# Projections of q, k, gate and v as 2x2x2 block products with seven products in place of eight

## The chip, the cores and the metric

One core of a Trainium2 chip runs the program. The metric is the device time of one execution in microseconds (us). TensorE (PE) multiplies, VectorE (DVE), ScalarE (ACT) and GpSimd (POOL) do the rest, SyncE (SP) starts most transfers. Each engine works off its own list of instructions in a fixed order.

## The reference

One layer of a hybrid trunk over 2048 rows of width 1024, all in float32. Cut to what matters:

```
hn   = rmsnorm(x, mix_norm_g)                    # 2048 x 1024
proj = hn @ w_in                                 # 1024 x 3072
u, g_ssm, q, k, v, g_attn = split(proj, 6 x 512)
y_ssm = s5_branch(u) * silu(g_ssm)               # diagonal complex SSM, scan, GELU, GLU
qh, kh = rmsnorm per head of 64                  # 8 heads
z = qh kh^T / 8, strictly causal, blocks of 128 queries
weights = exp(log_sigmoid(z) + sum of log_sigmoid(-z) over later keys)
y_att = (weights @ v) * silu(g_attn)
h = x + concat(y_ssm, y_att) @ w_out
out = h + sigmoid(rmsnorm(h, ple_norm_g) @ w_ple_gate) * (p @ w_ple_proj)
```

The change concerns `proj` without u: 2048 rows by 1024 times 1024 by 2560.

## The kernel before

A float32 product is made of three matmuls: each operand is split into a high part `hi` (a cast on ACT) and the remainder `lo` (a subtraction on DVE), and `mm3` or `mm3x` adds hi·hi, hi·lo and lo·hi in PSUM. 

The program has four stages:

- **u** (`phase_u`): RMSNorm of 16 row blocks of 128, the projection u, and the normalised rows, transposed and split, to DRAM as `hn_d` (1 MB a row block, hi and lo).
- **SSM**: eight batches (`ssm_pack`, `ssm_batch`). Beside each batch stands a `gate_unit`, which makes silu(g_ssm) for 256 rows with 96 matmuls of 256 columns. The last ones are followed by the first four row blocks of the attention projections. Six of the eight batches make their table `stC` (L332 to L334) on POOL, two on DVE.
- **Attention**: 40 steps `t`. The eight heads are four pairs `hp`, and pair `hp` starts at step 8·hp, so two pairs are under way at most times. `attn_block` (scores `ps_z`, DVE scan `px`, transposes `ps_wt`, ACT copy `ws`, output `ps_o`) does block t - 8·hp, and `attn_proj` makes the row block two steps ahead. At t = 30 to 39 the 16 GLU units (`ps_g`, `ps_v`) and, from t = 32, eight `cross_sums` are added: these make sums of blocks of `w_out` and `w_ple_gate` on POOL in tiles `old`, for the last stage.
- **out** (`phase_out`): both products with 1024x1024 weights, each already as 2x2x2 block products with seven products (`cross_products`).

`attn_proj` for one pair and one row block: one transfer of 1 MB from `hn_d` (`xt`, L717), 24 products of 128x128 by 512 columns, and `qn`, a 128x512 tile with q, k, gate and v of two heads. In 60 of the 64 row blocks each product is cut into two matmuls of 64 rows of the array, which run side by side into two PSUM tiles `ps_q` (L745); ACT copies the first (`part`, L751), DVE adds the second (`qn`, L65). In the first four blocks the whole array is used (`ps_qk`). v is shifted down by one row with two transfers (L753, L755) and subtracted on POOL.

The shape of a TensorE matmul is called its use of the array below: `ps_z`, `ps_wt`, `ps_tq` and `ps_q` take row halves (64*128 in the profile), `ps_o` takes column halves (128*64), and projections with the whole array are 128*128.

The order on each engine is not the order of the code. `arrange` passes all instructions with a cost for each through `best_order` and `list_schedule`, which build a list schedule, improve it in some turns and write the instructions in that order; a list cannot be changed at run time. Pools of SBUF are placed by `plan`.

Of the kernel before, what the change touches and what calls it, by code (L numbers as in the profile page):

```python
# [18 lines left out]
P = 128  # L19
# [21 lines left out]
XB, XTB, GTB, QSB, PXB, WSB, SWB, ROTB, STA, STB, STC, ALT, ALT0, ALT1, SSM_STEPS, SSM_DEPTH, PREP0, PXX, WSX, XTX, XT0 = 4, 2, 5, 5, 8, 5, 2, 2, 3, 2, 3, "o", 0, 30, 10, 2, 0, 0, 0, 0, 13  # L41
WE = 6
AHEAD = 4
BANKS = (("z0", "z1", "tr"), ("acc", "ssm"), ("o",)), (("z0", "z1"), ("acc", "tr"), ("o",)), (("z0", "z1"), ("acc", "ssm", "tr"), ("o",))
# [262 lines left out]
def ssm_pack(e, sm, R, b):  # L307
# [23 lines left out]
    gp = (nc.vector if b < 2 else nc.gpsimd).tensor_tensor  # L331
# [16 lines left out]
    lt = e.spare.tile([P, 512], F32, tag="part", name="lt", bufs=1)[:, :HS * P]  # L348
# [124 lines left out]
def load_w(e, blocks, width, scale, tag="w", pool=None, bufs=None, at=0, act=True, spare=None):  # L473
# [3 lines left out]
    for c, src in enumerate(blocks, at):  # L477
        t = (pool or e.wpool).tile([P, 2, width], F32R, tag=tag, name=f"w_{tag}", **({"bufs": bufs} if bufs else {}))
# [67 lines left out]
def phase_u(e, pool, xp, chain):  # L546
# [5 lines left out]
    def load_plain(T):  # L552
        xt = xp.tile([P, 2, 2, NC8, P], F32R, tag="xg", name="xt", bufs=2)
        w = []
        for hf in range(2):
            plain.append(pool.tile([P, NC8, P], F32, tag="x", name="x", bufs=XB))
        for c in range(0, NC8, 2):
            cs = slice(c, c + 2)
            for hf in range(2):
                x = plain[2 * T + hf]  # L560
                nc.sync.dma_start(x[:, cs], e.xt[2 * T + hf, :, cs])
                split(e, xt[:, hf, 0, cs], xt[:, hf, 1, cs], x[:, cs])
            if T == 0:
                w += load_w(e, row_blocks(e.w_in[0], NC8, 0)[cs], 512, e.gmix, act=ACT0, spare=pool, at=c)
        for hf in range(2):
            with e.later(1):
                nc.sync.dma_start(e.hn_d[2 * T + hf], xt[:, hf].rearrange("p s c t -> p (s c t)").bitcast(F32))
        return xt, w
# [19 lines left out]
    def load_x(T):  # L588
        xt = xp.tile([P, 2, 2, NC8, P], F32R, tag="xg", name="xt", bufs=2)
        for hf in range(2):  # L590
# [7 lines left out]
            nc.scalar.activation(x, x, AF.Copy, scale=rs)  # L598
            for h, ps in enumerate(turned(e, "ps_x", ("z0", "z1"), [x[:, c * P:(c + 1) * P] for c in range(NC8)])):
                d = slice(64 * h, 64 * h + 64)  # L600
                split(e, xt[:, hf, 0, :, d], xt[:, hf, 1, :, d], ps)
            nc.sync.dma_start(e.hn_d[2 * T + hf], xt[:, hf].rearrange("p s c t -> p (s c t)").bitcast(F32))
# [10 lines left out]
    for T in range(NT // 2):  # L613
        if 2 <= T + 1 < NT // 2:
            xts[T + 1] = load_x(T + 1)
        xt = xts.pop(T - 2, None)
# [25 lines left out]
def gate_unit(e, pool, w, T, xt):  # L642

    nc = e.nc
    if xt is None:
        xt = pool.tile([P, 2, 2, NC8, P], F32R, tag="xg", name="xg", bufs=2)
        for hf in range(2):
            nc.sync.dma_start(xt[:, hf].rearrange("p s c t -> p (s c t)").bitcast(F32), e.hn_d[2 * T + hf])
    for ct in range(4):
        o = e.bank("ps_sg", "o", "z0", "z1")[:, :256]  # L650
        for c in range(NC8):
            cs = slice(ct * P, (ct + 1) * P)
            mm3(e, o, (w[c][:, 0, cs], w[c][:, 1, cs]), (xt[:, :, 0, c], xt[:, :, 1, c]), c == 0, c == NC8 - 1)
        if T < 1:
            og = pool.tile([P, 256], F32, tag="sg", name="og", bufs=2)
            vt(nc, og, o, e.row[T], ALU.mult)
            o = og
        sg = pool.tile([P, 256], F32, tag="sg", name="sg", bufs=2)
        nc.scalar.activation(sg, o, AF.Sigmoid)
        vt(nc, sg, o, sg, ALU.mult)  # L660
        c0 = (T % 2) * 256
        nc.sync.dma_start(e.gs_d[T // 2][ct * P:(ct + 1) * P, c0:c0 + 256], sg)
    return xt


def glu_load(e, k):
    rows = e.w_glu[0].rearrange("(g h) n -> h g n", h=GH)
    return load_w(e, [rows[4 * c:4 * c + 4, :, 512 * k:512 * k + 512] for c in range(4)], 512, None)


def glu_z(e, pool, tb):

    zf = e.z_d.rearrange("j (k p) c -> p k j c", p=P)
    zr = pool.tile([P, 2, 4, 512], F32R, tag="zr", name="zr", bufs=1)
    for k in range(4):
        n = NCH // 4
        zt = pool.tile([P, L, n], F32, tag="zt", name="zt", bufs=3)
        e.nc.sync.dma_start(zt, zf[:, k, :, tb * n:(tb + 1) * n])
        hi, lo = (zr[:, s, k].rearrange("p (c j) -> p c j", j=L) for s in range(2))
        split(e, hi, lo, zt.rearrange("p j c -> p c j"))  # L680
    return zr


def glu_unit(e, old, slots, w, zr, tb, m):
    nc = e.nc
    both = old(slots[m % len(slots)])
    gt, sg = both[:, 0], both[:, 1]
# [4 lines left out]
    for half, ps in ((1, pg), (0, pv)):  # L692
        for c in range(4):
            wt = w[half][c]
            mm3(e, ps, (wt[:, 0, cs], wt[:, 1, cs]), (zr[:, 0, c], zr[:, 1, c]), c == 0, c == 3)
# [16 lines left out]
def attn_proj(e, pool, A, i, xt=None):  # L712

    nc = e.nc
    if xt is None:
        xt = e.xp.tile([P, 2, NC8, P], F32R, tag="xt", name="xt", bufs=XTB)
        e.xdma(xt.rearrange("p s c t -> p (s c t)").bitcast(F32), e.hn_d[i])  # L717
    both = pool.tile([P, 4 * HPP, HD], F32, tag="qn", name="qn", bufs=2)
    if i == 0:
        A.v[i] = e.kv_tile(A.hp, i, "v", [P, HPP, HD])  # L720
        nc.gpsimd.memset(A.v[i][:1], 0.0)
    if i + 1 < NT and i + 1 not in A.v:
        A.v[i + 1] = e.kv_tile(A.hp, i + 1, "v", [P, HPP, HD]) if i + 1 != AHEAD else pool.tile([P, HPP, HD], F32, tag="vl", name="vl", bufs=1)
    if A.v[i].tensor.name.startswith("vl"):
        row = A.v[i]
        A.v[i] = e.kv_tile(A.hp, i, "v", [P, HPP, HD])
        nc.sync.dma_start(A.v[i][:1], row[:1])
    flat, vb = both.rearrange("p h d -> p (h d)"), A.v[i].rearrange("p h d -> p (h d)")
    vr = flat[:, 384:]
    if len(e.q_banks) == 1:  # L730
        pq = e.bank("ps_qk", *e.q_banks)
        for c in range(NC8):
            mm3x(e, pq, (xt[:, 0, c], xt[:, 1, c]), (A.w[c][:, 0], A.w[c][:, 1]), c == 0, c == NC8 - 1)
        if i < 2:
            nc.scalar.activation(flat, pq, AF.Copy, scale=e.rs[i])
        else:
            nc.scalar.activation(flat, pq, AF.Copy)
    else:
        pq = [e.bank("ps_q", *e.q_banks) for h in range(2)]
        for c in range(NC8):  # L740
            with e.abreast():
                for s, (a, b) in enumerate(((0, 0), (0, 1), (1, 0))):
                    for h, o in enumerate(pq):
                        r = slice(64 * h, 64 * h + 64)
                        nc.tensor.matmul(o, xt[r, a, c], A.w[c][r, b], start=c + s == 0, stop=c == NC8 - 1 and s == 2)  # L745
        part = pool.tile([P, 512], F32, tag="part", name="part", bufs=1)
        if i < 2:
            nc.scalar.activation(part, pq[0], AF.Copy, scale=e.rs[i])
            stt(nc, flat, pq[1], e.rs[i], part, ALU.mult, ALU.add)
        else:  # L750
            nc.scalar.activation(part, pq[0], AF.Copy)  # L751
            vt(nc, flat, pq[1], part, ALU.add)
    nc.sync.dma_start(vb[1:], vr[:P - 1])  # L753
    if i + 1 < NT:
        nc.sync.dma_start(A.v[i + 1][:1].rearrange("p h d -> p (h d)"), vr[P - 1:])  # L755
    nc.gpsimd.tensor_tensor(vb, vr, vb, op=ALU.subtract)  # L756
# [19 lines left out]
    if len(e.q_banks) == 1:  # L776
# [73 lines left out]
def attn_pass(e, hp):  # L850
    A = Env()
    A.hp, A.k, A.v, A.q, A.w = hp, [], {}, {}, []
    return A


def attn_w(e, A, lo, hi, **kw):
    cols = e.w_in[0][:, 1024:].rearrange("(n p) (k c) -> n p k c", p=P, k=4)
    A.w += load_w(e, [cols[c, :, :, P * A.hp:P * (A.hp + 1)] for c in range(lo, hi)], 512, e.gmix, at=lo, **kw)
# [23 lines left out]
class Halves:  # L882
    def __init__(self, e):
        self.e, self.open = e, []

    def tile(self, shape, dt, **kw):
        if not self.open:
            t = self.e.xp.tile([P, 2, NC8, P], dt, tag="xt", name="wx", bufs=XTB)
            self.open = [t[:, k].rearrange("p c t -> p (c t)").rearrange("p (s n) -> p s n", s=2) for k in (1, 0)]
        return self.open.pop()  # L890
# [147 lines left out]
def phase_out(e, pool, far, wpool2, wo4):  # L1038
# [6 lines left out]
    e.wg = [cross_weights(e, e.w_pg[0], e.sg_d, e.gple, p, **(dict(pool=Halves(e)) if p == 4 else dict(tag="wc", pool=wpool2, bufs=8) if p > 4 else {})) for p in range(7)]  # L1045
# [5 lines left out]
def hybrid_block_kernel(ctx: ExitStack, tc: tile.TileContext, x, xt, small, p, w_in, ssm_w_glu, w_out, w_ple_gate,  # L1051
# [15 lines left out]
    e.hn_d = [scratch(f"hn{i}", [P, 2 * DM]) for i in range(NT)]  # L1067
# [96 lines left out]
    gx = pool(left, "gx")  # L1164
# [458 lines left out]
```

## Time and profile before

| | us |
|---|---|
| median of three runs | 1475.82 (1475.17 to 1476.36) |
| the profiled execution: time, span | 1474.24, 1472.5 |
| PE busy in the span | 1436.7 |
| DVE busy | 1009.0 |
| ACT busy | 810.4 |
| POOL busy | 474.8 |
| mean granted TensorE clock | 0.994 |

The span runs from the first to the last instruction; the time of that execution is 1.7 us longer. Busy times count overlapping instructions of an engine once. A matmul's duration in the profile is longer than the distance between the starts of two matmuls, because they are pipelined; where the work of PE is summed, the distance between starts is used and is called pitch.

The stages end near 129 us (u), 316 (SSM), 1093 (attention) and 1472 (out).

### The profile page before, as it was taken

How to read it: one execution, taken by the hardware profiler on the slowest of the kernel's cores; microseconds unless marked ns; L12 is line 12 of the kernel's file. 1: busy time of each engine (PE TensorE's matmuls, PEld its weight loads, DVE VectorE, ACT ScalarE, POOL GpSimd, SP SyncE). 2: the span in 40 equal slices, each digit the busy share in tenths (PEclk: the TensorE clock that was granted, in tenths of full speed). 3: DMA queues.
4: the chain of work that ended last, by engine and by line, in shares of the span. 5: the costliest groups of instructions: out<-in, count | busy, mean ns of one | idle time of the engine just before them, and what ended most of it. 6: DMA issues, size and time to landing. Idle time of an engine off the chain costs nothing.

```text
span 1472.5 us, 33586 instructions
## 1 busy us (share of the span) xinstructions
PE 1436.7 (98%) x13068; PEld 1224.2 (83%) x13068; DVE 1009.0 (69%) x1817; ACT 810.4 (55%) x1765; POOL 474.8 (32%) x512
## 2 busy tenths in 40 slices
PE   6999999999999999999999999999999999999998
PEld 5999889988888888888888877777778888778786
DVE  8953977977567786678766775666778557754444
ACT  5654555565555766567655665555665345533432
POOL 3131363522221211221121124443334554534432
PEclk8999999999999999999999999999999999999999
DMA  8886845645333433334332455766568556523221
GB/s 289 288 287 205 250 143 186 206 143 168 128 130 125 144 112 114 114 130 140 121 126 102 142 146 171 226 218 178 155 201 280 176 171 200 166 65 101 93 72 58
DMA packets 179054, 238.21 MB, mean 162 GB/s; under 512 B 65760, under 2 KB 121296, under 8 KB 167760
## 3 DMA queue, kind: packets, MB, share of 16 engines
q1 hardware_dynamic: 176512, 227.49, 48.0%
q0 software_dynamic: 2384, 8.59, 2.0%
q8 instruction: 103, 1.69, 0.5%
q14 instruction: 55, 0.45, 0.1%
HBM read 166.94 MB, written 64.90 MB: 157 GB/s over the span
## 4 chain that ended last, share of the span: by engine, by line
PE 81%; DVE 7%; DMA 3%; ACT 3%; issue 3%; POOL 2%; SPq 1%; POOLq 0%; DVEq 0%; ACTq 0%
PE ps_q L745 21%; PE ps_o L843 7%; PE ps_z L812 6%; PE ps_wt L526 4%; PE ps_g L707 4%; PE ps_h L709 4%; PE ps_h L707 3%; PE ps_h L708 3%; PE ps_g L709 3%; PE ps_g L708 3%; DMA v<-qn 2%; PE ps_u L541 1%; PE ps_u L543 1%; PE ps_u L542 1%; PE ps_sg L541 1%
## 5 line engine op out<-in xcount | busy, mean ns | idle before, releaser
L821 DVE TENSOR_TENSOR_SCAN px<-px,ps_z 128x512 f32<-128x512 f32 (+3 forms) x320 | 339.9, 1086 | 85.9 <-ACT px L816 61.0
L745 PE MATMUL ps_q<-w_w,xt 64*128 64x512 f32 x2784 | 376.7, 399 | 1.3 <-DVE qn L65 0.7
L745 PEld LDWEIGHTS ps_q<-w_w,xt 64*128 64x128 f32 x2784 | 270.8, 185 | 39.7 <-DVE qn L65 2.2
L816 ACT ACTIVATE px<-ps_z 128x512 f32<-128x512 f32 (+3 forms) x320 | 159.2, 535 | 81.0 <-PE ps_z L812 79.8
L835 ACT ACTIVATE ws<-ps_wt 128x512 f32<-128x512 f32 (+3 forms) x320 | 160.7, 539 | 72.0 <-PE ps_wt L526 67.1
L812 PE MATMUL ps_z<-k,q 64*128 64x512 f32 (+3 forms) x960 | 137.7, 379 | 3.7 <-DVE px L821 1.8
L843 PE MATMUL ps_o<-ws,v 128*64 128x128 f32 x2176 | 134.9, 276 | 0.0
L843 PEld LDWEIGHTS ps_o<-ws,v 128*64 128x64 f32 x2176 | 117.3, 137 | 17.6 <-issue 14.7
L507 POOL TENSOR_TENSOR rs_qk<-rs_qk,mhalf 128x4 f32<-128x4 f32 x64 | 67.7, 1058 | 150.7 <-DVE rs_qk L72 148.1
L526 PEld LDWEIGHTS ps_wt<-ident,px 64*128 64x128 f32 x2176 | 95.5, 138 | 24.3 <-ACT ws L835 5.2
L812 PEld LDWEIGHTS ps_z<-k,q 64*128 64x128 f32 x960 | 87.9, 186 | 21.7 <-issue 5.4
L526 PE MATMUL ps_wt<-ident,px 64*128 64x64 f32 x2176 | 100.7, 224 | 2.0 <-ACT ws L835 1.8
L819 POOL TENSOR_SCALAR_AFFINE_SELECT px<-px 128x128 f32<-128x128 f32 x128 | 40.7, 328 | 164.2 <-ACT px L816 154.3
L756 POOL TENSOR_TENSOR v<-qn,v 128x128 f32<-128x128 f32 x64 | 32.2, 503 | 167.6 <-DMA v<-qn 153.9
L541 PE MATMUL ps_u<-xt,w_w 128*128 128x256 f32 x256 | 76.0, 298 | 7.5 <-ACT w_w L491 6.2
L65 DVE TENSOR_TENSOR yr<-sx,yr 128x512 fp32r<-128x512 f32 x64 | 50.6, 814 | 42.2 <-ACT yr L513 41.8
L543 PE MATMUL ps_u<-xt,w_w 128*128 128x256 f32 x256 | 74.5, 297 | 1.9 <-DVE w_w L76 1.8
L542 PE MATMUL ps_u<-xt,w_w 128*128 128x256 f32 x256 | 75.3, 295 | 0.5 <-DVE xt L65 0.5
L1032 POOL TENSOR_TENSOR sg<-sg,h 128x512 f32<-128x512 f32 x28 | 40.1, 1437 | 92.1 <-DVE sg L65 91.9
L513 ACT ACTIVATE yr<-sx 128x512 fp32r<-128x512 f32 x64 | 39.1, 627 | 53.7 <-POOL sx L912 22.6
L65 DVE TENSOR_TENSOR qn<-ps_q,part 128x512 f32<-128x512 f32 x54 | 36.8, 682 | 42.6 <-ACT part L751 39.0
L513 ACT ACTIVATE yr<-yq 128x512 fp32r<-128x512 f32 x48 | 30.2, 629 | 53.3 <-PE ps_h L709 24.5
(438 smaller groups left out, 3486.5 us busy)
## 6 DMA issues: line engine op xcount, KB each, us to landing
xt<-hn SPq DMA_DIRECT2D x58, 1024.0 KB
hn<-xt SPq DMA_DIRECT2D x16, 1024.0 KB
h<-h SPq DMA_DIRECT2D x64, 256.0 KB
wst<-in_w_in_dram SPq DMA_DIRECT2D x48, 256.0 KB
xg<-hn SPq DMA_DIRECT2D x12, 1024.0 KB
out_dram<-sg SPq DMA_DIRECT2D x31, 256.0 KB
x<-in_x_dram SPq DMA_DIRECT2D x14, 512.0 KB
h<-in_x_dram SPq DMA_DIRECT2D x28, 256.0 KB
```

The costliest lines, as they stand in the source:

```text
L526: e.nc.tensor.transpose(ps[h][:, 64 * k:64 * k + 64], v[r], e.ident[r, r])
L541: mm(out, wh, xh, start=first, stop=False)
L542: mm(out, wh, xl, start=False, stop=False)
L543: mm(out, wl, xh, start=False, stop=last)
L707: mm(out, xh, wh, start=first, stop=False, skip_group_check=more)
L709: mm(out, xl, wh, start=False, stop=last, skip_group_check=more)
L745: nc.tensor.matmul(o, xt[r, a, c], A.w[c][r, b], start=c + s == 0, stop=c == NC8 - 1 and s == 2)
L812: nc.tensor.matmul(z[:, :n], q[half[h], a], A.k[ch][half[h], b, :n], start=s == 0, stop=s == 2)
L816: nc.scalar.activation(px[:, :n], z[:, :n], AF.Sigmoid, scale=-(HD ** -0.5))
L821: nc.vector.tensor_tensor_scan(rv, rv, z[:, :n][:, ::-1], initial=1.0 if carry[h] is None else carry[h], op0=ALU.mult, op1=ALU.bypass)
L835: nc.scalar.activation(dst, ps, AF.Copy, bias=1.0, scale=-1.0)
L843: nc.tensor.matmul(po[half[h], :P], A.v[sb][:, h], w[:, h, b], start=sb == i, stop=sb == 0)
```

## The change

`attn_proj` goes. The projections q, k, gate and v of two head pairs (1024 columns, `pr` 0 and 1) and rows k and k+8 (two row blocks) become one 2x2x2 block product by Winograd's form: blocks are 128 rows by 512 of the inner dimension by 512 columns. Seven block products of 12 matmuls each replace eight, all with the whole array. `cross_cell` does it in three cells for each of 8 k: "first" (products 0 and 4), "middle" (1, 2, 5, 3) and "last" (6). Partial sums wait in DRAM (`r_d`, `n_d`) between cells, results go to `proj_d`, and `attn_prep` loads `qn` and the shifted v from there.

```diff
+def pair_weights(e, tag, pr, p):
+    src = e.w_in[0][:, 1024 * (pr + 1):1024 * (pr + 2)]
...
+    if p in (0, 4, 5):
...
+        return load_w(e, [block(i, j, c) for c in range(4)], 512, None, tag=tag)
...
+        gp = (nc.gpsimd if pr else nc.vector).tensor_tensor
+        raw, b = (raw_block(*ij) for ij in (((1, 1), (0, 1)) if p == 3 else ((0, 1), (0, 0))))
+        gp(raw, raw, b, op=ALU.subtract)
+        for ij in {1: ((1, 1),), 6: ((1, 1), (1, 0))}.get(p, ()):
+            q = raw_block(*ij)
+            gp(q, q, raw, op=ALU.subtract)
+            raw = q
+        split(e, t[:, 0], t[:, 1], raw)
...
+def cross_cell(e, ring, kind, pr, k, banks):
...
+    if kind == "first":
+        xs = [chunks(parted(e, half(e, a), None, pr)) for a in (a11, a12)]
+        ps = e.bank("ps_c", *banks)
+        product(ps, 0, xs[0], True)
+        put(e.r_d[k], ps)
+        product(ps, 4, xs[1], False)
+        put(out[0][0], ps)
+        if pr == 0:
+            gate_block(e, ring, k, xs, banks)
+    elif kind == "middle":
+        f1, g1, f2, f4 = (e.raw() for _ in range(4))
+        for f, a in ((f1, a21), (g1, a22), (f2, a11), (f4, a12)):
+            nc.sync.dma_start(f, a)
+        f3 = e.raw()
+        for o, a, b, op in ((f3, f2, f1, ALU.subtract), (f1, f1, g1, ALU.add), (f2, f1, f2, ALU.subtract), (f4, f4, f2, ALU.subtract)):
+            (nc.gpsimd if pr else nc.vector).tensor_tensor(o, a, b, op=op)
+        s2, s1, s4, s3 = (chunks(parted(e, e.quarter(), f, pr)) for f in (f2, f1, f4, f3))
+        m = get(e.r_d[k])
+        ps = e.bank("ps_c", *banks)
+        product(ps, 1, s2, True)
+        vt(nc, m, ps, m, ALU.add)
...
+        product(ps, 2, s1, True)
+        t = put(None, ps, m)
+        product(ps, 5, s4, False)
+        put(out[0][1], ps, m)
...
+        product(ps, 3, s3, True)
+        put(out[1][1], ps, t)
+        vt(nc, m, ps, m, ALU.add)
+        nc.sync.dma_start(e.n_d[k], m)
+    else:
+        n = get(e.n_d[k])
...
+        product(ps, 6, chunks(parted(e, half(e, a22), None, pr)), True)
+        put(out[1][0], ps, n)
...
-    gp = (nc.vector if b < 2 else nc.gpsimd).tensor_tensor
+    gp = nc.vector.tensor_tensor
...
-def attn_proj(e, pool, A, i, xt=None):
...
+def attn_prep(e, pool, A, i):
+    both = pool.tile([P, 4 * HPP, HD], F32, tag="qn", name="qn", bufs=2)
+    flat = both.rearrange("p h d -> p (h d)")
+    nc.sync.dma_start(flat, e.proj_d[A.hp][i * P:(i + 1) * P])
...
+        nc.sync.dma_start(vb, e.proj_d[A.hp][i * P - 1:(i + 1) * P - 1, 384:])
...
-            c = t - glu_at - 2
+            c = t - steps + 8
```

`parted` makes hi on ACT and lo on DVE (pr 0) or POOL (pr 1). The raw tiles `ra` have 7 buffers, the split tiles `xh` 5, the results `po` 4 and the loaded sums `ld` 3. The "first" cells of pr 0 stand in the SSM stage, two a batch, with the silu gate (`gate_block`: 24 matmuls of 512 columns for 128 rows, rows on partitions, then four transposes); the rest stands in the attention at the steps of a list `DUE`: middle of pr 0 at t = 0 to 4, last of pr 0 at 5 to 10, first of pr 1 at 7 to 12, middle of pr 1 at 13 to 20, last of pr 1 at 21 to 28. `hn_d` holds plain rows (512 KB a block), the norm's weight is applied to them and no longer to the weights of the other projections, and two row blocks are made a second time for it. `stC` is made on DVE in all batches. The third set of weights of the last stage (`wo4`) is loaded after the attention.

The scheduler makes new lists from this. **PE in the first third of the attention** (`ps_q` is the projection, `ps_tq` the transposes of q, k and gate). Before:

```order
L745 MATMUL ps_q<-w_w,xt 128x512 x24
L526 MATMUL ps_tq<-ident,qn 128x64 x4
L526 MATMUL ps_tq<-ident,gn 128x64 x2
L745 MATMUL ps_q<-w_w,xt 128x512 x6
L812 MATMUL ps_z<-k,q 128x512 x6
L745 MATMUL ps_q<-w_w,xt 128x512 x18
L526 MATMUL ps_wt<-ident,px 128x64 x8
L812 MATMUL ps_z<-k,q 128x512 x6
L843 MATMUL ps_o<-ws,v 64x128 x10
L745 MATMUL ps_q<-w_w,xt 128x512 x6
```

and in the changed kernel, in the stretch where the cells of pr 0 run (`ps_c` is the block product):

```order
L864 MATMUL ps_c<-w_w,xh 128x512
L865 MATMUL ps_c<-w_w,xh 128x512
L531 MATMUL ps_wt<-ident,px 128x64 x16
L866 MATMUL ps_c<-w_w,xh 128x512
L864 MATMUL ps_c<-w_w,xh 128x512
L865 MATMUL ps_c<-w_w,xh 128x512
L866 MATMUL ps_c<-w_w,xh 128x512
L864 MATMUL ps_c<-w_w,xh 128x512
L865 MATMUL ps_c<-w_w,xh 128x512
L531 MATMUL ps_tq<-ident,qn 128x64 x4
L531 MATMUL ps_tq<-ident,gn 128x64 x2
L938 MATMUL ps_z<-k,q 128x512 x6
```

Where the projection stood between other row-half work, whole-array matmuls now stand. Counted over the lists between the first `ps_z` and the first matmul of the last stage, the number of changes between the three uses of the array goes from 188 to 580, those into the whole array from 29 to 221.

**DVE at the start of the attention**, before (`px` is the scan, `qn<-ps_q,part` the sum of the halves):

```order
L65 TENSOR_TENSOR qn<-ps_q,part 128x512
L65 TENSOR_TENSOR yat<-ps_o,g 128x128
L821 SCALAR_TENSOR_TENSOR px<-px,ps_z 128x384 x2
L764 TENSOR_REDUCE ssq<-sq 128x4
L65 TENSOR_TENSOR gn<-qn,gn 128x128
L72 TENSOR_SCALAR rs_qk<-ssq 128x4
L65 TENSOR_TENSOR qn<-qn,rs_qk 128x256
```

and in the changed kernel, where the operands of a middle cell of pr 0 are made (L799 the sums of raw tiles, L663 the remainders, L734 the differences of weights):

```order
L799 TENSOR_TENSOR ra<-ra 128x512 x2
L890 TENSOR_REDUCE ssq<-sq 128x4
L799 TENSOR_TENSOR ra<-ra 128x512
L734 TENSOR_TENSOR wst<-wst 128x512
L663 TENSOR_TENSOR xh<-ra,xh 128x512
L70 TENSOR_TENSOR gn<-qn,gn 128x128
L77 TENSOR_SCALAR rs_qk<-ssq 128x4
L70 TENSOR_TENSOR w_v<-wst,w_v 128x512
L70 TENSOR_TENSOR yat<-ps_o,g 128x128
L663 TENSOR_TENSOR xh<-ra,xh 128x512
```

One addition a row block has given way to sums and remainders that read SBUF twice, between the small steps of `attn_prep`.

**POOL in the last steps**, before (`old` at L874 to L877 is a `cross_sums`, at L698 a GLU unit):

```order
L874 TENSOR_TENSOR old<-old 128x512
L875 TENSOR_TENSOR old<-old 128x512
L876 TENSOR_TENSOR old<-old 128x512
L877 TENSOR_TENSOR old<-old 128x512
L507 TENSOR_TENSOR rs_qk<-rs_qk,mhalf 128x4
L698 TENSOR_TENSOR old<-old 128x512
L756 TENSOR_TENSOR v<-qn,v 128x128
L819 AFFINE_SELECT px<-px 128x128 x2
```

and in the changed kernel:

```order
L995 TENSOR_TENSOR old<-old 128x512
L945 AFFINE_SELECT px<-px 128x128 x2
L996 TENSOR_TENSOR old<-old 128x512
L997 TENSOR_TENSOR old<-old 128x512
L998 TENSOR_TENSOR old<-old 128x512
L882 TENSOR_TENSOR v<-qn,v 128x128
L945 AFFINE_SELECT px<-px 128x128
L512 TENSOR_TENSOR rs_qk<-rs_qk,mhalf 128x4
```

The sums stand between the attention's own POOL steps in both; the GLU units have moved to other tiles and start at the same step.

More of the change, by code (lines that the diff above doesn't have):

```diff
@@ L639, in phase_u, with half @@
     return prep, xts
-def gate_unit(e, pool, w, T, xt):
-    nc = e.nc
[L645 to L663, printed above, removed]
+def half(e, src):
+    t = e.quarter()
+    e.nc.sync.dma_start(t[:, 1].bitcast(F32), src)
+    return t
@@ L1210, in hybrid_block_kernel @@
         last = g
[L1211 to L1213 removed]
+    for _ in range(SMIDDLE):
+        cell(("o", "z0", "z1"))
     list(last)
+    for i in range(AHEAD):
+        attn_prep(e, ap1, A[0], i)
+    e.alone = False
     right.close()
```

316 lines of the change are left out of this document (192 added, 124 removed).

## The prediction

> **What bounds the kernel now.** I read the page first (busy times, chain), then the busy times by stage, then the starts of matmuls in the timeline, then the groups by shape.
>
> ```profile
> span 1472.5 us, 33586 instructions
> PE 1436.7 (98%) x13068; PEld 1224.2 (83%) x13068; DVE 1009.0 (69%) x1817; ACT 810.4 (55%) x1765; POOL 474.8 (32%) x512
> ...
> PE 81%; DVE 7%; DMA 3%; ACT 3%; issue 3%; POOL 2%; SPq 1%; POOLq 0%; DVEq 0%; ACTq 0%
> ```
>
> TensorE is busy 98% and carries 81% of the chain that ended last. The next view cuts the span at the stages' ends (columns: stretch, its length, busy time and instructions of PE, PEld, DVE, ACT, POOL, then clock, DMA share, GB/s; the attention is cut at 916, where the third head pair gives out its last block).
>
> ```profile
> 0.00:129.00 129.00, 114.61 (x1004) 109.50 (x1005) 91.27 (x357) 72.07 (x128) 35.64 (x47) 0.95 0.80 276
> 129.00:316.00 187.00, 182.87 (x1470) 172.18 (x1471) 152.40 (x265) 103.83 (x237) 74.94 (x43) 1.00 0.61 188
> 316.00:916.00 600.00, 595.36 (x7244) 504.84 (x7243) 420.91 (x728) 361.17 (x878) 126.58 (x230) 1.00 0.42 133
> 916.00:1093.00 177.00, 172.00 (x1647) 136.88 (x1643) 116.92 (x153) 107.42 (x214) 73.02 (x73) 0.99 0.63 191
> 1093.00:1472.00 379.00, 371.87 (x1716) 300.79 (x1712) 227.48 (x316) 165.88 (x310) 164.60 (x120) 1.00 0.44 142
> ```
>
> In the SSM stage and the attention PE idles 14 us of 964; DVE is at 81% and 69%, POOL at 40% and 26%, the clock at full speed. So the time there is PE's work plus what PE spends between instructions. Busy time is a poor measure of work, as durations overlap; I price matmuls by the distance of their starts.
>
> ```profile
> 1104.04 0.39 PE L708 MATMUL ps_h<-w_w,yr 128*128 128x512 f32 x1
> ...
> 1112.20 0.39 PE L708 MATMUL ps_h<-w_w,yr 128*128 128x512 f32 x1
> 617.60 3.02 PE L745 MATMUL ps_q<-w_w,xt 64*128 64x512 f32 x24
> 620.46 0.28 PE L526 MATMUL ps_tq<-ident,qn 64*128 64x64 f32 x4
> 303.06 0.28 PE L541 MATMUL ps_sg<-xg,w_w 128*128 128x256 f32 x1
> ...
> 304.13 0.28 PE L541 MATMUL ps_sg<-xg,w_w 128*128 128x256 f32 x1
> ```
>
> Between the first two rows lie 36 starts: 8.16/36 = 0.2267 us; within groups I see 0.2265 to 0.2285, and take 0.2285 beside other work. A row half costs 2.86/24 = 0.119, so that two halves (0.238) already cost about what a whole-array matmul does. 256 columns: 1.07/9 = 0.119.
>
> **PE's work, part by part.**
>
> ```profile
> L745 PE MATMUL ps_q<-w_w,xt 64*128 64x512 f32 x2784 | 376.7, 399 | 1.3 <-DVE qn L65 0.7 <-ACT part L751 0.5 <-DVE old L76 0.2
> L745 PE MATMUL ps_q<-w_w,xg 64*128 64x512 f32 x96 | 12.3, 397 | 1.6 <-DVE gsq L65 1.6
> L541 PE MATMUL ps_sg<-xg,w_w 128*128 128x256 f32 x192 | 55.6, 290 | 0.0
> L707 PE MATMUL ps_qk<-w_w,xg 128*128 128x512 f32 x32 | 12.9, 403 | 0.0
> L1000 PE MATMUL ps_t<-ident,h 128*128 128x128 f32 x128 | 19.4, 272 | 0.0
> ```
>
> - Attention: 2880 row halves go (2784 + 96), 2880 x 0.119 = 343 us. There come 8 rows k x 12 products (all but the first cells of pr 0) x 12 matmuls = 1152 x 0.2285 = 263. Difference -80.
> - SSM: the first cells of pr 0 bring 192 x 0.2285 = 44; the four early row blocks (96 in the three groups `ps_qk`) take away 22. The silu gate has 384 x 0.2285 = 88 for 768 x 0.119 = 91 (192 and 64 in each of three lines), plus 64 transposes at 19.4/128 = 0.15, 10. Sum 44 - 22 + 88 - 91 + 10 = +29.
> - Stage u: two row blocks normalised again, 32 small transposes, +1.
>
> That is -50: what seven products in place of eight give after the gate, the unsplit shape and the transposes.
>
> **What PE spends between shapes.** The trace of before has changes of the array's use, most of them between row and column halves. A GLU stretch shows those into and out of the whole array:
>
> ```profile
> 931.90 0.68 PE L526 MATMUL ps_wt<-ident,px 64*128 64x64 f32 x16
> 932.51 0.50 PE L542 MATMUL ps_g<-zr,w_w 128*128 128x512 f32 x1
> 932.85 0.40 PE L543 MATMUL ps_g<-zr,w_w 128*128 128x512 f32 x1
> 933.09 0.40 PE L541 MATMUL ps_g<-zr,w_w 128*128 128x512 f32 x1
> ...
> 936.08 0.39 PE L542 MATMUL ps_v<-zr,w_w 128*128 128x512 f32 x1
> 936.40 0.71 PE L526 MATMUL ps_wt<-ident,px 64*128 64x64 f32 x16
> 936.92 0.60 PE L812 MATMUL ps_z<-k,q 64*128 64x256 f32 x6
> ```
>
> Sixteen transposes take 0.52 when the next group has their shape (936.40 to 936.92) and 0.61 before a whole-array matmul: 0.09. The first whole-array matmul takes 0.34 where the next ones take 0.23 to 0.24: 0.11. The last one before transposes takes 0.32: 0.09. A round trip costs 0.29 us. The order lists have 221 entries into the whole array in the attention where there were 29: 192 x 0.29 = 56 us. Bounds: 0.09 a round trip if only one gap counts and the others vanish under PE's other waits, 17; the same places read over all such changes give medians up to 0.35, 67. I take 56, nearest to the rows, since the round trips stand in the same company (transposes, scores) as these. The Trainium skill ("TensorEngine Tiling (Array Packing)", section Key Properties) says that a change of the tiling mode drains TensorE, which these gaps bear out; "TensorE: Matmul & The Clock Gate" (section Single matmul latency) puts a drain at about 0.175 us, by which 392 more changes would cost an estimated 69 us, a quarter more than by the rows.
>
> **The other engines.**
>
> ```profile
> L65 DVE TENSOR_TENSOR qn<-ps_q,part 128x512 f32<-128x512 f32 x54 | 36.8, 682 | 42.6 <-ACT part L751 39.0 <-PE ps_z L812 3.5
> L65 DVE TENSOR_TENSOR sg<-ps_p,sg 128x512 f32<-128x512 f32 x31 | 21.4, 691 | 20.4 <-ACT sg L1030 17.8 <-PE ps_p L709 1.9
> L65 DVE TENSOR_TENSOR w_w<-wst,w_w 128x512 fp32r<-128x512 f32 x36 | 26.3, 748 | 6.8 <-ACT w_w L513 6.8
> L65 DVE TENSOR_TENSOR yr<-yq,yr 128x512 fp32r<-128x512 f32 x48 | 48.0, 999 | 9.5 <-ACT yr L513 7.4 <-DMA yq<-ys 2.0
> L332 DVE TENSOR_TENSOR stC<-pwr,cts 128x1024 f32<-128x1024 f32 x2 | 2.4, 1220 | 0.0
> L912 POOL TENSOR_TENSOR sx<-yq 128x512 f32<-128x512 f32 x28 | 37.5, 1338 | 10.5 <-ACT yq L1002 10.5
> L874 POOL TENSOR_TENSOR old<-old 128x512 f32<-128x512 f32 x8 | 10.3, 1290 | 50.4 <-ACT old L870 27.4 <-DMA old<-in_w_out_dram 23.0
> ```
>
> DVE in the attention: 60 sums of halves go (-41); there come 96 additions from PSUM (six for each of 16 cell triples, 0.69: +66), 72 sums and remainders of operands of pr 0 (0.75: +54), and of the 52 additional weight remainders and differences about half (+20). That makes 538 + 99 = 637 us. POOL gets as many operand steps for pr 1, 88 x 1.34 = 118, and 28 differences of weights, 38: 200 becomes some 355. By my pitches and gaps PE's work there fills 754 of the stage's 777 us; it becomes 754 - 80 + 56 = 730. DVE then has 87% of it, where it had 69%. ACT gets 32 + 24 copies and casts more, all under 70%.
>
> DVE in the SSM stage: 18 products for `stC` (+22), 16 remainders of first cells (+12), the weights of pr 0 and the gate's (+10): 152 becomes 196, against PE's 183 + 29 = 212.
>
> Waits to be added, each with its bounds:
>
> - Stage u: 16 small splits where the weight now goes on the rows, +1 (0 to 3).
> - SSM, DVE at 92%: before, at 81%, PE lost 4 us of 187. +8 (0 to 20).
> - Start of the attention: a middle cell's loads stand in SP's list behind the last stores of `z`; then three sums, a cast and a remainder, 5 x 0.75 and the transfer, about 8 us with 4 to 5 us of other PE work. Net +4 (0 to 10).
> - Attention from t = 5 to 29, two heavily used engines beside PE: +2. Lower bound -10 (PE idles little there now, so little can be won), upper bound below as a rival.
> - Tail: PE's work after 916 falls from 161 by my pitches (172 busy) to about 100, so that the scans and POOL's `cross_sums` stand alone. Eight cycles of four `old` sums at 1.3 and transfers of the same chain take 14 to 16 us each (POOL waits 50 us for ACT and DMA in eight groups, 6 a cycle): 112 to 128. The attention's POOL steps stand among them in a fixed list. +8 (0 to 20).
> - Transfers: `hn_d` shrinks to half, `proj_d`, `r_d` and `n_d` come; the share is 42% in the attention. Loads run ahead of use: 0. If that cover goes, `qn` is late by one transfer a block.
>
> Sum: -50 + 56 + 23 = +29. On the profiled execution's 1474.24 (span 1472.5 and 1.7 around it; 1.6 below the median of the runs) this gives 1503; I forecast 1503.
>
> **The rivals.**
>
> *R1, faster.* The round trips cost less than I think: the gaps into the whole array fall together with waits which a list this mixed has anyway, or vanish where the neighbour is a long group. At 0.09 a round trip and half of the waits, -50 + 17 + 11 = -22: 1452. The point from which it decides is (50 - 23)/192 = 0.14 us a round trip with my waits, 0.20 with half of them. For it: PE's present time is 23 us above work and gaps, so part of what I count as wait may be gap. Against it: the rows at 931.90 to 936.92 are not waits; the profile names no releaser there.
>
> *R2, slower still.* Operands bound the cells. The middle cell has 48 matmuls, 11.0 us of PE, and asks of pr 0 eight DVE steps in SBUF and five additions, 8 x 0.75 + 5 x 0.69 = 9.4 us, of pr 1 eight POOL steps, 8 x 1.34 = 10.7 us, through 7 raw and 5 split buffers. The next cell's tiles come free only as this one's products end. Steps of DVE with two SBUF inputs cost 0.999 in the last stage, where POOL is busy 43%, and 0.748 for weights; at +0.25 each and 2 to 4 us of slip in each of 16 cells it adds 20 to 70: 1520 to 1570, most likely 1535. The Trainium skill ("SBUF - State Buffer", section Who interferes with whom) has a rule for it: such a step and a POOL step that reads SBUF lock each other out. The rows (999 against 691 with one PSUM input) agree. Against R2: pr 1's middle cells come one a step of some 19 us (777/40), nearly twice what their operands take; pr 0's eight come in five steps, one in 12 us.
>
> *R3, no difference.* Gains and gaps cancel and hardly any wait is added: -50 + 56 - 3 = about 0, 1476. It needs DVE at 87% not to delay PE.
>
> **How the numbers follow.** My forecast (1485 to 1520) 0.52, R1 0.24, R3 0.08, R2 0.16. Two runs of this kernel can be told apart from about 0.2%, 3 us. R1 is faster with all of its 0.24; R3 is within 0.2% with 0.06 and faster with 0.02; the rest is slower: 0.26, 0.06, 0.68. To leave out no more than 2 in 10 the range cuts R1 below 1452 (half of it, 0.12) and R2 above 1535 (half, 0.08): 1452 to 1535; the forecast's own range is 1485 to 1520.
>
> **What would show it.** In the profile of the changed kernel: first `ps_c` after transposes takes 0.34 and not 0.23 (the gaps); the SSM stage ends near 355, the attention near 1120, the last stage is 379 long; DVE busy near 1160 and POOL near 610; PE waits for `xh` less than 20 us in all, else R2; matmuls of the middle cells come in bursts of 0.23 without gaps at shape changes, then R1. I would be wrong above all if PE's idle time in the attention rises by more than 40 us (waits for operands I have priced at almost nothing), or if the 1152 matmuls of `ps_c` have another pitch than 0.2285.

## The result: slower by 5.2%, and the profile after

The changed kernel takes 1551.29 us (median of 4 runs, 1550.1 to 1555.05), the kernel before 1475.69 on the same chip: ratio 1.0516, 95% interval 1.0498 to 1.0535. The forecast of 1503 has the sign right, but less than half of the size, and the time lies above its range. The profiled execution has a span of 1548.3 us, 75.8 more than before. The page of the changed kernel, with its chain:

```profile
span 1548.3 us, 30655 instructions
PE 1476.1 (95%) x11148; PEld 1159.3 (75%) x11148; DVE 1163.2 (75%) x2027; ACT 876.2 (57%) x1877; POOL 577.1 (37%) x612
...
PE 81%; DVE 7%; ACT 5%; issue 4%; POOL 2%; DMA 2%; SPq 0%; ACTq 0%; DVEq 0%; POOLq 0%
```

PE has 1920 instructions fewer and is busy longer. The stages, in the columns of the prediction's second view:

```profile
0.00:145.00 145.00, 122.45 (x1043) 116.43 (x1044) 114.32 (x389) 78.33 (x133) 30.39 (x47) 0.91 0.60 196
145.00:356.00 211.00, 207.22 (x1228) 173.92 (x1226) 166.59 (x285) 123.28 (x257) 30.23 (x26) 0.99 0.62 183
356.00:1167.00 811.00, 775.01 (x7171) 568.44 (x7170) 654.40 (x1036) 506.95 (x1176) 356.50 (x422) 0.98 0.55 171
1167.00:1548.00 381.00, 371.44 (x1712) 300.55 (x1710) 227.90 (x320) 167.60 (x313) 160.02 (x117) 1.00 0.44 143
```

Stage u grows by 16 (to 145 from 129), SSM by 24, the attention by 34, the last stage by 2. In the attention PE stands idle 36 us where it stood idle 10 before, and the clock is no longer full.

For the attention I split the stretch into PE's work (matmuls by pitch), changes of shape (each priced by the medians of its kind in these traces) and a rest. Before: 777 = 731 + 25 + 21. After: 811 = 652 + 93 + 66. So the block products give back 79 us, as forecast, and changes of shape cost 68 and the rest, waits in the main, 45 more. (Some records are missing from the traces; work is by the full counts.)

Where these 45 us lie, a cut into the first 40 us, the middle and the last 100 us shows, first before and then after:

```profile
316.00:356.00 40.00, 38.82 (x434) 33.43 (x433) 27.48 (x56) 24.52 (x63) 10.44 (x22) 1.00 0.55 180
356.00:993.00 637.00, 631.93 (x7590) 532.69 (x7587) 442.57 (x742) 382.18 (x912) 154.23 (x248) 1.00 0.44 141
993.00:1093.00 100.00, 96.62 (x869) 75.59 (x867) 67.78 (x84) 61.90 (x118) 34.93 (x34) 0.98 0.57 168
```

```profile
356.00:396.00 40.00, 30.43 (x158) 20.93 (x156) 33.38 (x68) 19.93 (x53) 8.43 (x15) 0.79 0.68 216
396.00:1067.00 671.00, 651.43 (x6016) 479.52 (x6017) 541.98 (x868) 412.85 (x967) 293.48 (x350) 0.99 0.54 163
1067.00:1167.00 100.00, 93.15 (x1004) 67.99 (x1001) 79.04 (x103) 74.16 (x157) 54.58 (x57) 0.97 0.62 203
```

PE's idle time grows by 8, 14 and 4 us, 26 in all. What a lower clock costs is estimated as PE's busy time by the share of the clock that is missing: 6, 7 and 3 us after, 0, 0 and 2 before, 14 more (lost clock below). Both together grow by 14 us at the start, 21 in the middle and 4 at the end; some 5 of the 45 are left without a place. PE's waits in the attention, before and after (columns: us in total, times, longest):

```profile
PE ps_wt L526 <- ACT ws L835: 1.8, 4, 0.6
PE ps_z L812 <- DVE px L821: 1.8, 2, 1.6
```

```profile
PE ps_wt L531 <- ACT ws L961: 10.0, 11, 1.8
PE ps_z L938 <- DVE px L947: 7.3, 6, 2.3
PE ps_c L864 <- DVE po L70: 3.8, 3, 1.7
PE ps_c L864 <- ACT xh L662: 1.8, 2, 1.2
```

All waits of `ps_c`, for PSUM tiles, operands and weights, come to 8.5 us; nearly all the others, some 26 us, are waits for the attention's own steps.

What a change of shape costs can be read from a piece of PE's timeline in the attention of the changed kernel:

```profile
703.35 0.71 PE L531 MATMUL ps_wt<-ident,px 64*128 64x64 f32 x16
703.87 0.94 PE L938 MATMUL ps_z<-k,q 64*128 64x512 f32 x6
704.74 0.50 PE L865 MATMUL ps_c<-w_w,xh 128*128 128x512 f32 x1
705.08 0.40 PE L866 MATMUL ps_c<-w_w,xh 128*128 128x512 f32 x1
705.31 0.39 PE L864 MATMUL ps_c<-w_w,xh 128*128 128x512 f32 x1
705.63 0.71 PE L531 MATMUL ps_wt<-ident,px 64*128 64x64 f32 x16
```

Six score matmuls take 0.87 where 6 x 0.119 is 0.71 (0.16 into the whole array), the first `ps_c` takes 0.34 for 0.23 (0.11), the last one 0.32 (0.09): 0.36 for a round trip, in which these three whole-array matmuls stand.

### The profile page after: what moved, and what is told of

Its sections match the earlier page's. It is cut to its first block, busy times and chain, and to the rows that moved or that the text cites. A ratio compares the mean times of both kernels' runs of the same rounds, so it can differ in the third digit from the quotient of the medians.

```text
span 1548.3 us, 30655 instructions
## 1 busy us (share of the span) xinstructions
PE 1476.1 (95%) x11148; PEld 1159.3 (75%) x11148; DVE 1163.2 (75%) x2027; ACT 876.2 (57%) x1877; POOL 577.1 (37%) x612
## 4 chain that ended last, share of the span: by engine, by line
PE 81%; DVE 7%; ACT 5%; issue 4%; POOL 2%; DMA 2%; SPq 0%; ACTq 0%; DVEq 0%; POOLq 0%
PE ps_o L969 8%; PE ps_z L938 7%; PE ps_c L864 7%; PE ps_c L866 7%; PE ps_c L865 7%; PE ps_wt L531 5%; PE ps_g L864 3%; PE ps_g L866 3%; PE ps_g L865 3%; PE ps_h L864 3%; PE ps_h L865 3%; PE ps_h L866 3%; PE ps_sg L866 1%; PE ps_sg L865 1%; PE ps_sg L864 1%
## 5 line engine op out<-in xcount | busy, mean ns | idle before, releaser
L938 PE MATMUL ps_z<-k,q 64*128 64x512 f32 (+3 forms) x960 | 145.7, 399 | 10.2 <-DVE px L947 7.3
L969 PE MATMUL ps_o<-ws,v 128*64 128x128 f32 x2176 | 143.6, 282 | 0.0
L969 PEld LDWEIGHTS ps_o<-ws,v 128*64 128x64 f32 x2176 | 120.6, 140 | 20.2 <-issue 15.2
L531 PEld LDWEIGHTS ps_wt<-ident,px 64*128 64x128 f32 x2176 | 83.9, 141 | 56.1 <-ACT ws L961 21.4
L938 PEld LDWEIGHTS ps_z<-k,q 64*128 64x128 f32 x960 | 79.9, 190 | 46.5 <-issue 22.7
L864 PE MATMUL ps_c<-w_w,xh 128*128 128x512 f32 x224 | 91.8, 413 | 5.2 <-DVE po L70 3.3
L866 PE MATMUL ps_c<-w_w,xh 128*128 128x512 f32 x224 | 91.8, 411 | 0.8 <-DVE xh L663 0.7
L865 PE MATMUL ps_c<-w_w,xh 128*128 128x512 f32 x224 | 91.4, 408 | 0.7 <-DVE w_w L70 0.7
L546 PE MATMUL ps_u<-xt,w_w 128*128 128x256 f32 x256 | 77.0, 306 | 10.1 <-ACT w_w L518 5.9
L547 PE MATMUL ps_u<-xt,w_w 128*128 128x256 f32 x256 | 77.1, 304 | 0.9 <-DVE xt L70 0.7
L548 PE MATMUL ps_u<-xt,w_w 128*128 128x256 f32 x256 | 75.0, 304 | 3.1 <-DVE w_w L70 2.5
L662 ACT ACTIVATE xh<-ra 128x512 fp32r<-128x512 f32 x64 | 39.3, 632 | 56.1 <-PE ps_c L866 36.3
L882 POOL TENSOR_TENSOR v<-qn,v 128x128 f32<-128x128 f32 x64 | 31.8, 497 | 96.2 <-DMA qn<-proj 78.5
```

What stands on the lines that cost most here:

```text
L531: e.nc.tensor.transpose(ps[h][:, 64 * k:64 * k + 64], v[r], e.ident[r, r])
L546: mm(out, wh, xh, start=first, stop=False)
L547: mm(out, wh, xl, start=False, stop=False)
L548: mm(out, wl, xh, start=False, stop=last)
L864: mm(out, xh, wh, start=first, stop=False, skip_group_check=more)
L865: mm(out, xh, wl, start=False, stop=False, skip_group_check=more)
```

## The experiments

Every ratio is to the kernel before in runs on the same chip, with its 95% interval. The scheduler makes new lists after every edit, so each figure below is that of an edit together with its new order. The runs are named e1 to e13; there is no e6.

**The changes of shape by themselves (e3).** The kernel before, with the 60 halved row blocks of the attention made with the whole array: no block products, no cells, no DRAM.

```diff
-        pq = [e.bank("ps_q", *e.q_banks) for h in range(2)]
...
+        pq = e.bank("ps_q", *e.q_banks)
+        for c in range(NC8):
+            mm3x(e, pq, (xt[:, 0, c], xt[:, 1, c]), (A.w[c][:, 0], A.w[c][:, 1]), c == 0, c == NC8 - 1)
```

> The kernel before with the 60 halved row blocks of the attention made with the whole array: 1440 matmuls for 2880 row halves, no sum on DVE, no cells and no DRAM. By pitches PE's work changes by 1440 x 0.2285 - 343 = -14 us; entries into the whole array go from 29 to 187. Theory S (changes of shape cost 0.38 us a round trip, as the changed kernel's trace has them): -14 + 158 x 0.38 = +46, 1522. By the forecast's 0.29: +32, 1508. Rival (round trips are cheap and operands or waits made the change slow): -14 + 158 x 0.09 = 0, 1476, or less as DVE is relieved of 41 us.

1518.7 us, ratio 1.0291 (1.0272 to 1.0311). First scores and first matmuls of the last stage (duration least, median and most in ns, first and last start), and then the attention's busy times, in this kernel's trace:

```profile
L805 PE MATMUL ps_z<-k,q x960: 269/392/504, 318.4 to 1130.7; 64*128 64x512 f32 x133, 64*128 64x384 f32 x22, 64*128 64x128 f32 x20, 64*128 64x256 f32 x17
L707 PE MATMUL ps_h<-w_w,yr x128: 387/389/499, 1133.4 to 1285.2; 128*128 128x512 f32 x128
```

```profile
318.00:1133.00 815.00, 804.38 (x7430) 608.38 (x7431) 508.32 (x818) 470.28 (x1090) 199.56 (x302) 1.00 0.44 138
```

The attention takes 815 us, 38 more than before, with PE hardly idle (11 us), a full clock and DVE at 62%. With 14 us less work, 158 more entries cost 52: 0.33 us each, with no cells and no idle time of PE to explain them. The changed kernel's 192 more entries are then 63 us.

**Fewer changes.** The kernel of e3 with the 24 matmuls of a row block kept together (e12, 109 entries for 187), and the changed kernel with the 12 of a product kept together in the same way (e4, 162 for 221). The edit of the first:

```diff
+        with e.abreast():
+            for c in range(NC8):
+                mm3x(e, pq, ...)
```

> The kernel of e3 (the kernel before, projections with the whole array) with the 24 matmuls of each row block kept together: entries into the whole array 109 for 187, the work the same. Theory S at the 0.33 us a round trip that e3 gave: -78 x 0.33 = -26, 1493. Rival (e3 is slow for another reason than its round trips, such as the size of its matmuls or their order): within 5 us of e3's 1519, or above it as the bursts of 5.5 us hold up the scans.

> The changed kernel with the 12 matmuls of each block product kept together in PE's list: entries into the whole array 162 in place of 221. Theory S: 59 x 0.38 = 22 us less, 1529. By 0.29: 1534. Rival (round trips cheap): within 5 us of 1551; if the products' last operand then holds up PE, above 1551.

They take 1597.8 (1.0823, 1.0787 to 1.0859) and 1585.07 us (1.0737, 1.0719 to 1.0754): both slower than the kernels they were made from, by 79 and 34. In the first, changes of shape fall from 79 us to 56 in my sum, as theory S has it, and the rest grows by about 100: PE idles 77 us in the attention where it idled 11 in e3, and the clock is 0.98 there. PE's waits and one place of its timeline show what is missing:

```profile
PE ps_wt L526 <- ACT ws L829: 45.8, 47, 6.5
PE ps_tq L526 <- ACT ws L829: 11.4, 19, 1.3
...
769.77 0.46 PE L526 MATMUL ps_wt<-ident,px 64*128 64x64 f32 x8 [1.45 <-ACT ws L829]
```

Before, the first of these waits came to 1.8 us. With 24 matmuls in one burst of 24 x 0.2267 = 5.4 us, none of them is left to stand between the attention's other groups; there PE finds the PSUM tile of the transposes still to be copied by ACT. In the changed kernel (e4) the changes fall from 93 to 75 us, and in the last 90 us of its scores PE idles 20 us at a clock of 0.81 (6 us at 0.96 without the edit):

```profile
1103.00:1193.00 90.00, 69.95 (x805) 54.49 (x803) 65.17 (x89) 63.05 (x139) 42.05 (x46) 0.81 0.53 176
```

So the round trips are no accident of the order: they are what it pays so that PE has something to do while scans and copies run. Theory S missed that side in both; the rivals' last clauses allow for a slower kernel, but give no size. As the waits grew by more than the changes fell, these two runs say nothing on the price of a change, which rests on e3 and on the rows of the timelines.

**Stage u.** Among the lines of the change that the core shown above leaves out are two which the prediction did not price: the descriptor memory of POOL's transfers is set to 4096 bytes, and `plan` lets the pools start 12288 bytes lower. ACT and POOL in the changed kernel:

```profile
94.11 1.16 POOL L647 DMA_DIRECT2D u<-uq  x1 [8.11 <-issue]
95.29 0.57 POOL L512 TENSOR_TENSOR rs_x<-rs_x,mhalf 128x1 f32<-128x1 f32 x1
95.90 1.15 ACT L603 ACTIVATE x<-x,rs_x 128x1024 f32<-128x1024 f32 x1 [10.46 <-POOL rs_x L512]
```

(in brackets the idle time before and what ended it). POOL stands 8 us before it issues a store of u, with nothing that the profile shows to wait for; RMSNorm's power step is next in its list, and ACT waits 10.5 us for that. The stores of u in the kernel before have no such idle time. Two experiments: the kernel before with that memory cut (e2), and the changed kernel with the eight stores on SP (e1).

```diff
-    nc = _bacc.Bacc("TRN2", target_bir_lowering=False, num_devices=1)
+    nc = _bacc.Bacc("TRN2", target_bir_lowering=False, num_devices=1, dynamic_dma_scratch_size=4096)
```

> The kernel before with that descriptor memory alone cut to 4096 bytes. Theory A: the first stage grows by 8 to 16 us, 1484 to 1492, with idle time 'issue' before POOL's stores of u. Rival B: 1476, no change.

```diff
-                nc.gpsimd.dma_start(e.u_d[ct]...
+                nc.sync.dma_start(e.u_d[ct]...
```

> The changed kernel with the 8 stores of u in the first stage started by SP in place of POOL. Theory A (POOL's transfers wait for room in a descriptor memory that the change cut from 16384 to 4096 bytes, and RMSNorm's power steps stand behind them on POOL): the first stage loses 10 of its 16 added us, POOL's idle time of 16 us 'issue' before L647 is gone, and the time falls from 1551 to 1537-1542. Rival B (DVE's multiplication by the norm's weight makes the stage long): within 3 us of 1551.

The first takes 1484.7 us (1.0056, 1.0037 to 1.0074), and its trace has the same wait:

```profile
95.81 1.16 POOL L638 DMA_DIRECT2D u<-uq  x1 [9.14 <-issue]
96.98 0.56 POOL L507 TENSOR_TENSOR rs_x<-rs_x,mhalf 128x1 f32<-128x1 f32 x1
```

The last matmul of `ps_u` starts at 138.3 there (128.9 before). The second takes 1547.73 us (1.0483, 1.0466 to 1.0501), where theory A expected 1537 to 1542: the wait is gone and the stage ends at 139 for 144, which is 4 to 5 us in the time. So theory A holds, for part of the stage's growth. The next experiment (e9) leaves out the norm's weight on the rows (a copy on ACT in place of DVE's multiplication):

```diff
-                vt(nc, xv[:, :, 64 * h:64 * h + 64], ps, e.gmix.unsqueeze(2).to_broadcast([P, NC8, 64]), ALU.mult)
+                nc.scalar.activation(xv[:, :, 64 * h:64 * h + 64], ps, AF.Copy)
```

> The kernel of e1 with the multiplication of the normalised rows by the norm's weight on DVE replaced by a copy on ACT; the weight is left out of the computation there. Theory D (what is left of the first stage's growth, 139 against 129 us, is DVE's added steps and their place in the chain of a row block): the stage falls to 130-133, 1539-1542. Rival (the extra row blocks and the rows' stores): it stays, 1548.

1542.95 us (1.0450, 1.0434 to 1.0465), the stage ends at 134. The multiplication on DVE is 5 us of the stage; another 5, the two row blocks made again among them, were not taken apart.

**Waits in the attention.** SP's list waits longest for the buffer of a `qn` load, in the changed kernel:

```profile
SPq L874 <- PE ps_tq L531: 101.1, 45, 7.8
```

Row, weight and `zt` loads stand behind it. Such a wait need not cost anything: in the kernel before, SP stood longer for the buffers of the row blocks, while PE idled 10 us in the whole attention:

```profile
SPq L717 <- PE ps_q L745: 119.6, 32, 7.4
```

Three buffers for two (e5):

```diff
-    both = pool.tile([P, 4 * HPP, HD], F32, tag="qn", name="qn", bufs=2)
+    both = pool.tile([P, 4 * HPP, HD], F32, tag="qn", name="qn", bufs=3)
```

> The kernel of e1 with three buffers of qn in place of two. Theory Q (SP stands up to 7.8 us, 101 us in all, before a load of qn whose buffer is still read by PE, and loads of rows, weights and z stand behind it; their users hold up the lists of DVE and ACT): PE's rest in the attention outside of work and changes of shape falls by 10 to 25 us of some 75, 1523-1538. Rival: these loads come in time anyway, within 4 us of 1548.

1535.72 us, ratio 1.0409 (1.039 to 1.0428), 0.0074 less than e1's. The rest in the attention falls by 20 us, and its trace has

```profile
SPq L874 <- PE ps_tq L531: 86.6, 40, 7.8
```

so SP still waits there; against e1 (96.2 us, 42 times) little of that wait is gone. What fell is PE's idle time in the attention, from 37 to 29 us, and the clock rose from 0.97 to 0.99, an estimated 13 us. The size is as theory Q has it, but that it comes through SP's list is not shown. The sums of the rows left out (e10), to see what the operand steps cost:

```diff
-        f3 = e.raw()
-        for o, a, b, op in (...):
-            (nc.gpsimd if pr else nc.vector).tensor_tensor(o, a, b, op=op)
+        f3 = g1
```

> The kernel of e1 without the four sums of row blocks in each middle cell (loaded rows are used in their place, so the products are of other operands): 32 steps less on DVE, 24 us, and 32 on POOL, 43 us; PE's work is the same, entries into the whole array 208 for 221. Rival R2 of the prediction (operand steps in SBUF and their chain hold up PE): 1500-1525. Theory S (work and changes of shape, then waits of other kinds): -13 x 0.33 = -4 and a few us of relief, 1535-1545.

1530.9 us, 1.0369 (1.0353 to 1.0384), 17 us less than e1, between the two theories: 4 us below theory S's range and 6 above R2's. By my sum some 14 of them are rest and the others changes of shape. Two sets of tiles for `cross_sums` (e7):

```diff
-    rows = [b[:, k] for b in (old(2), old(5)) for k in range(2)]
+    rows = [b[:, k] for b in ((old(6), old(7)) if c % 2 else (old(2), old(5))) for k in range(2)]
```

> The kernel of e1 with the eight cross_sums of the last steps alternating between two sets of tiles in place of one. Theory R3 of the prediction (the chain of cross_sums holds up POOL's and SP's lists in the last steps): the stretch from 1100 to the end of the attention loses 8 to 15 us, 1533-1540. Rival: it is not on the path, within 4 us of 1548.

1541.92 us, 1.0441 (1.0425 to 1.0457): 6 us less, but not where the expectation has it (it calls the tail term of the prediction's sum R3). In the last 100 us of the scores PE idles 13 us at a clock of 0.91, where e1 has 6 at 0.97: worse, not better. The new order has 195 entries for 221, and 26 x 0.33 = 9. Both together (e11):

> e5 and e7 together: stores of u from SP, three buffers of qn, two sets of tiles for cross_sums. If the two effects are separate (1.0483 to 1.0409 and to 1.0441), the ratio to the kernel before is 1.0483 - 0.0074 - 0.0042 = 1.037, 1532 on this scale; if they are the same wait seen twice, 1.041. Neither theory has it below 1.02, since the changes of shape remain (entries 193).

1524.91 us, 1.0330 (1.031 to 1.035), the best of the changed kernels, and the effects add up to a little more than their sum (1.037 was expected). With products kept together (e13) it loses again:

> e11 with the 12 matmuls of a block product kept together as in e4: entries 166 for 193. Theory S: -27 x 0.33 = -9 against e11. If bursts of 2.7 us hold up the scans or the last steps, as e4 was 34 us slower than the changed kernel, it is slower than e11 by 10 to 30; with two sets of tiles in the last steps less of that should be left.

1564.97 us, 1.0598 (1.058 to 1.0617): 40 us more than e11, and more than the 10 to 30 expected.

**The start of the attention.** PE's timeline of the changed kernel, and then windows of 8 us with the clock (the number after POOL's):

```profile
359.63 0.33 PE L905 MATMUL ps_tq<-ident,gn 128*128 128x128 f32 x1 [2.30 <-DVE gn L70]
361.07 1.29 PE L938 MATMUL ps_z<-k,q 64*128 64x256 f32 x6 [1.12 <-ACT k L914]
...
369.13 2.52 PE L938 MATMUL ps_z<-k,q 64*128 64x512 f32 x6 [1.78 <-ACT k L914]
...
373.03 0.80 PE L864 MATMUL ps_c<-w_w,xh 128*128 128x512 f32 x1 [1.16 <-ACT xh L662]
...
374.05 0.63 PE L864 MATMUL ps_c<-w_w,xh 128*128 128x512 f32 x1
374.48 0.63 PE L865 MATMUL ps_c<-w_w,xh 128*128 128x512 f32 x1
...
377.95 0.40 PE L864 MATMUL ps_c<-w_w,xh 128*128 128x512 f32 x1
378.19 0.40 PE L865 MATMUL ps_c<-w_w,xh 128*128 128x512 f32 x1
```

```profile
360.00:368.00 8.00, 4.14 (x15) 2.60 (x15) 5.77 (x15) 4.93 (x15) 3.09 (x8) 0.54 0.98 333
368.00:376.00 8.00, 5.66 (x24) 3.31 (x26) 7.02 (x15) 4.67 (x12) 3.07 (x4) 0.50 0.67 209
376.00:384.00 8.00, 8.00 (x57) 5.94 (x53) 6.41 (x12) 2.33 (x6) 0.51 (x1) 0.89 0.54 156
```

The first block product starts 17 us after the first scores (356.2), PE is idle 6 of 16 us, and what it does runs at half clock: the starts of `ps_c` lie 0.43 us apart at 374, where the clock is 0.50, and 0.24 at 378. The clock falls at about 361, after idle times of 2.30 and 1.12 us with 0.33 us of work between them, and it is full again from about 378, when PE has worked for 4.7 us without a break. The Trainium skill ("TensorE: Matmul & The Clock Gate", section "Part 1: The HAM clock gate") says that the clock is halved after an idle window of about 3.4 us and full after about 3.4 us of sustained work; the trace agrees on the two speeds and comes near both times, though the idle time came in two pieces here, the longer of 2.3 us. To bring the operands earlier, three rows of the first middle cell were loaded into tiles free in the SSM stage (e8):

```diff
+        if (pr, k) == (0, 0):
+            with e.first():
+                f1, g1, f2 = (get(a) for a in (a21, a22, a11))
...
```

> e11 with three of the four row loads of the first middle cell into tiles that are free during the SSM stage, so that they no longer wait for the memory of that stage and for the stores of z ahead of them in SP's list. Theory M (PE idles at the start of the attention for these operands and then runs at half clock): the first 40 us lose some 10 of their 15 to 17 us of rest, the granted clock there is nearer 1, the ratio falls by 0.005 to 0.008 against e11. Rival (the attention's own first steps hold it up): no change from e11.

1531.7 us, 1.0375 (1.0354 to 1.0396): 7 us more than e11. The first product now starts at 361.9, 10 us after the first scores, but those wait for `px` and `k` all the same, and the clock is at 0.50 from 360 to 364. In the first 40 us PE idles 10 us as in e11, at a clock of 0.91 for 0.79; in the 14 us before them the clock is 0.63 where e11 has 0.88, so that the lost clock has in part only moved. The attention's own first steps hold up its start as much as the operands do; the rival was nearer.

## Why the prediction was wrong, point by point

- **PE's work**: right. The attention's work falls by 79 us (80 forecast), at the pitch that was taken. The SSM stage grows by 24 where 29 of work and 8 of waits were forecast: DVE is busy 167 us there, not 196, and PE idles 4 us as before, so the 8 were not paid.
- **Changes of shape**: right in kind, 56 forecast, 63 to 68 measured (0.33 each in e3 for 0.29). The low end of 0.09 is excluded by e3, and R1 with it: PE was not idle there, so the entry cost is no wait.
- **The other engines**: totals right (DVE 1163 for 1160, POOL 577 for 610; DVE in the attention 654 for 637).
- **Waits to be added**: the step that failed, in three of its terms.
  - Stage u was given +2 (1 of work, 1 of waits) and grew by 16. The cut of the descriptor memory, a line of the diff, was not counted as an edit (5 to 9 us, e1 and e2), and the weight's multiplication was counted as 16 small splits (5 us, e9).
  - The start of the attention was given +4; idle time and lost clock grew by 14.
  - The middle was given +2, "two heavily used engines beside PE", with no row for its size; idle time and lost clock grew by 21. PE had idled little because its filler needed no operand steps. Now these steps stand in the lists of ACT, DVE and POOL beside those of the attention, and PE waits in the main for the attention's own: 10.0 us for ACT's copies `ws` (1.8 before), 7.3 for the scan (1.8). A third buffer of `qn` (e5) or four sums less a cell (e10, 14 us of rest) takes part of it away. Which list hands on the delay is not shown.
- **Half clock**: missing from the prediction, a term put at nothing; an estimated 14 of the 45 us. It also hid the sign that was named: PE's idle time in the attention rose by 26 us and not by more than 40, as work at half clock counts as busy.
- **Luck**: the SSM stage ends at 356, as forecast (355), because stage u was 14 us too short in the sum and the SSM stage 13 too long.
- **R2**: the time lies in its range (1520 to 1570), but its own sign did not come: PE waits 2.5 us for `xh` in all, where 20 were to decide. The price that it puts on DVE's steps is there, but small. Of these rows of DVE steps with two SBUF inputs (count, busy us, mean ns), the first meets a step of POOL only 2 times in 32, the other two more often:

```profile
L663 DVE TENSOR_TENSOR xh<-ra,xh 128x512 fp32r<-128x512 f32 x32 | 21.3, 688 | 0.3 <-ACT xh L662 0.2
L70 DVE TENSOR_TENSOR w_w<-ra,w_w 128x512 fp32r<-128x512 f32 x16 | 14.8, 929 | 1.0 <-ACT w_w L518 1.0
L70 DVE TENSOR_TENSOR w_w<-wst,w_w 128x512 fp32r<-128x512 f32 x13 | 11.6, 900 | 5.7 <-ACT w_w L518 5.7
```

  Those steps of the last two rows that overlap no step of POOL take 0.69 at most. So the slowing beside POOL bears out R2, but in these rows it is 16 x 0.24 + 13 x 0.21 = 7 us of DVE's time in the whole attention, and R2, with its slip in each cell, asked for 20 to 70.
- **Tail chain** (R3 of the expectations, +8 in the sum): idle time and lost clock grew by 4 us in the last 100, and a second set of tiles (e7) did not shorten them; that the chain of `cross_sums` is on the path is not shown.

The 45 us are divided by place and by kind, but not by cause: e5, e10 and the start overlap, every edit came with a new order, and no run took all of them away. e11 is still 3.3% slower than the kernel before, and no run points to a version that beats it: seven products save 79 us in the attention, their cells cost 63 in changes of shape and 24 in the SSM stage, so that nothing would be won even without the waits.

## What to carry to other kernels

Before whole-array work is mixed into half-array work, count the entries that the order will have and price them by a pair of rows; and expect that packing the matmuls into bursts to save entries may cost more in waits than it saves. Work that fills an engine's gaps is only a filler if it asks little of the other engines' lists, since the steps whose waits it is to cover stand in them too: ask for each of its operands which list it stands in, behind what, and what then stands behind it. Idle time of TensorE that comes in a row of short pieces can cost the clock too, so price it at more than its length. Price every line of a diff, memory sizes too, by the stage in which the resource is used, not by the stage that the change is about.

## What the runs showed of the hardware that was not expected

- Cutting the descriptor memory of POOL's transfers to 4096 bytes (the pools could start 12288 bytes lower) made POOL stand 8.1 and 9.1 us before one issue in two kernels, with no releaser in the profile, and cost the kernel before 0.56%.
- Entering and leaving the whole array among row-half work costs 0.33 us a time over 158 of them, while PE's idle time in the attention stays at 11 us (10 before).
- Keeping 24 matmuls together, with the same work and 109 entries for 187, made a kernel 79 us slower.
